# The state-space branch of a hybrid decoder block: two blocks of 128 steps scanned once, in place of sixteen blocks of 16 scanned twice

## The chip, the cores and the metric

The kernel runs on one core of a Trainium2 chip. The metric is the device time of one execution in microseconds (us). The core's engines are TensorE (PE in the rows, with its weight loads as PEld), VectorE (DVE), ScalarE (ACT), GpSimd (POOL) and SyncE (SP), which here issues the transfers. Each engine works through its own list of instructions in order and waits on semaphores for the others.

## The reference

For 256 tokens of width 2048 the block computes an RMS norm, one wide projection, two token mixers side by side, a gated merge, an output projection, and a mixture of experts with a final norm. The change touches one of the mixers, the state-space branch:

```
u = proj[:, :512]                       # 32 groups of 16 channels, 64 states each
lam_bar = exp(lam * step)               # complex, per state
bu = einsum(b_bar, u)                   # complex input of each state
s[t] = lam_bar * s[t-1] + bu[t]         # 256 steps
y = real(einsum(c, s)) + d * u
out = gelu(y) * sigmoid(gelu(y) @ w_glu + b_glu)
```

## The kernel before, in words

The 2048 states are 16 slices of 128 partitions, four slices to a chunk; `s5_chunk(c)` does one chunk. `lam_bar` is `rho` times a rotation. The kernel turns the input back by the rotation's angle, so that real and imaginary part become two real recurrences with factor `rho`, scans them on VectorE, and turns the result forward again. The tables of the angle reach 16 steps (`loc_c`, `loc_s`), and those of a block's angle 16 blocks (`blk_c`, `blk_s`); `powers` (L360) builds both by doubling.

A chunk works on two slices at a time (half a chunk). Per slice two small matmuls (L422) put the input into a `mid` bank of PSUM (two banks); six VectorE instructions of 256 elements (L430 to L435) turn it back into `bz`. A first scan (L444, real and imaginary, 512 elements each) runs inside each block of 16, with zeros in `d_loc` at each block's start. Eighteen instructions of 32 or 30 elements (L453 to L477) then work out what each block hands to the next, and add it to the blocks' first elements. The same scan runs a second time, six instructions of 512 elements turn the result forward (L483 to L488), and four matmuls (L493) take it to the outputs; each chunk ends with L495.

Around this stands the other mixer. In a loop of four batches of three heads, every projection unit is 1 MB of weights (`in_unit`, L398), of which ScalarE rounds each half (`whi`, L99) and VectorE takes the rest (`wlo`, L100); each half feeds 24 matmuls of 256 columns (L104 to L106), three for each block of weights. `lru_head` and `lru_tail` hold the second mixer's own VectorE, ScalarE and GpSimd work, `xl` (L536) among it, for which a matmul waits. After the loop come two more chunks, the projections by `w_plru` (L602, 36 matmuls a tile), by `w_in` (L613), `w_glu` and `w_ps5`, then `w_out` (L726) and the experts (L886 on), whose weights arrive by L704. Before the chunks, four pairs of transposes (L352) turn `bpad`, which VectorE builds (L341 to L345).

The order on every engine is fixed when the program is built: a scheduler with a clock of its own places the instructions, and the loads, roundings and differences of weights go ahead of all else (`high_priority`). The code's order decides only between the rest. A tile with one buffer makes its next user wait until the last reader is done.

Of the kernel before, what the change touches and what calls it, by code (L numbers as in the profile page):

```python
# [9 lines left out]
F32 = mybir.dt.float32  # L10
F32R = mybir.dt.float32r
# [24 lines left out]
def block_kernel(  # L36
# [268 lines left out]
    blk_c = tb_.tile([P, 16, LOC], F32, name="blk_c")  # L305
    blk_s = tb_.tile([P, 16, LOC], F32, name="blk_s")
# [53 lines left out]
    def powers(tc_, ts_):  # L360
        V.memset(tc_[:, :, 0], 1.0)
        V.memset(ts_[:, :, 0], 0.0)
        n = 1
        while n < 16:
# [12 lines left out]

    powers(loc_c, loc_s)
# [4 lines left out]
    V.tensor_tensor(rho16, rho, rho, op=ALU.mult)  # L383
    for _ in range(3):
        V.tensor_tensor(rho16, rho16, rho16, op=ALU.mult)
    d_loc = tb_.tile([P, 16, 16], F32, name="d_loc")
    d_blk = tb_.tile([P, 16, 16], F32, name="d_blk")
    V.tensor_copy(d_loc, rho[:, :, None].to_broadcast([P, 16, 16]))
    V.tensor_copy(d_blk, rho16[:, :, None].to_broadcast([P, 16, 16]))
    V.memset(d_loc[:, :, 0], 0.0)  # L390
    V.memset(d_blk[:, :, 0], 0.0)
# [16 lines left out]

    def s5_chunk(c):
        yps[c] = aux_bank()  # L410
        SB = 2
        for sb in range(4 // SB):
            bz = mp.tile([P, 2, SB, T], F32, tag="bz", bufs=2, name=nm("bz"))
            gz = mp.tile([P, 2, SB, T], F32, tag="gz", bufs=2, name=nm("gz"))
            s0 = 4 * c + sb * SB
            for i in range(SB):
                s = s0 + i
                q = s % 4
                rows = slice(32 * q, 32 * q + 32)
# [9 lines left out]
                bzv = bz[:, :, i, :].rearrange("p r (j t) -> p r j t", t=16)
                V.tensor_tensor(ttv[:, 0], p3[:, 1], ls, op=ALU.mult)  # L430
                V.tensor_tensor(ttv[:, 1], p3[:, 0], ls, op=ALU.mult)
                V.tensor_tensor(bzv[:, 0], p3[:, 0], lc, op=ALU.mult)
                V.tensor_tensor(bzv[:, 1], p3[:, 1], lc, op=ALU.mult)
                V.tensor_tensor(bz[:, 0, i, :], bz[:, 0, i, :], tt[:, 0], op=ALU.add)
                V.tensor_tensor(bz[:, 1, i, :], bz[:, 1, i, :], tt[:, 1], op=ALU.subtract)  # L435
            d3 = mp.tile([P, SB * T], F32, tag="d3", bufs=1, name=nm("d3"))
            A.activation(d3.rearrange("p (s j t) -> p s j t", s=SB, t=16),
                         d_loc[:, s0:s0 + SB, None, :].to_broadcast([P, SB, 16, 16]), AF.Copy)
            bz4 = bz.rearrange("p r s (j t) -> p r s j t", t=16)
            gz4 = gz.rearrange("p r s (j t) -> p r s j t", t=16)  # L440

            def scan():
                for ri in range(2):
                    V.tensor_tensor_scan(gz[:, ri].rearrange("p s t -> p (s t)"), d3,  # L444
                                         bz[:, ri].rearrange("p s t -> p (s t)"), 0.0, op0=ALU.mult, op1=ALU.add)

            scan()

            w = lambda: mp.tile([P, SB, 16], F32, tag="cw", bufs=8, name=nm("cw"))
            bc, bs = blk_c[:, s0:s0 + SB, 0:16], blk_s[:, s0:s0 + SB, 0:16]  # L450
            gr, gi = gz4[:, 0, :, :, 15], gz4[:, 1, :, :, 15]
            t1, t2, yr, yi, vr, vi = w(), w(), w(), w(), w(), w()
            V.tensor_tensor(yr, gr, bc, op=ALU.mult)  # L453
            V.tensor_tensor(t1, gi, bs, op=ALU.mult)
            V.tensor_tensor(yi, gi, bc, op=ALU.mult)
            V.tensor_tensor(t2, gr, bs, op=ALU.mult)
            V.tensor_tensor(yr, yr, t1, op=ALU.add)
            V.tensor_tensor(yi, yi, t2, op=ALU.subtract)
            fl = lambda t: t.rearrange("p s j -> p (s j)")
            db = fl(d_blk[:, s0:s0 + SB, :])  # L460
            V.tensor_tensor_scan(fl(vr), db, fl(yr), 0.0, op0=ALU.mult, op1=ALU.add)
            V.tensor_tensor_scan(fl(vi), db, fl(yi), 0.0, op0=ALU.mult, op1=ALU.add)
            bc, bs = blk_c[:, s0:s0 + SB, 1:16], blk_s[:, s0:s0 + SB, 1:16]
            v_r, v_i = vr[:, :, 0:15], vi[:, :, 0:15]
            t1, t2, yr, yi = w(), w(), w(), w()
            t1, t2, yr, yi = t1[:, :, 0:15], t2[:, :, 0:15], yr[:, :, 0:15], yi[:, :, 0:15]
            V.tensor_tensor(yr, v_r, bc, op=ALU.mult)
            V.tensor_tensor(t1, v_i, bs, op=ALU.mult)
            V.tensor_tensor(yi, v_i, bc, op=ALU.mult)
            V.tensor_tensor(t2, v_r, bs, op=ALU.mult)  # L470
            V.tensor_tensor(yr, yr, t1, op=ALU.subtract)
            V.tensor_tensor(yi, yi, t2, op=ALU.add)
            rb = rho[:, s0:s0 + SB, None].to_broadcast([P, SB, 15])
            V.tensor_tensor(yr, yr, rb, op=ALU.mult)
            V.tensor_tensor(yi, yi, rb, op=ALU.mult)
            V.tensor_tensor(bz4[:, 0, :, 1:16, 0], bz4[:, 0, :, 1:16, 0], yr, op=ALU.add)
            V.tensor_tensor(bz4[:, 1, :, 1:16, 0], bz4[:, 1, :, 1:16, 0], yi, op=ALU.add)  # L477
            scan()
            lc = loc_c[:, s0:s0 + SB, None, 0:16].to_broadcast([P, SB, 16, 16])
            ls = loc_s[:, s0:s0 + SB, None, 0:16].to_broadcast([P, SB, 16, 16])  # L480
            tr = mp.tile([P, SB, T], F32, tag="st", bufs=2, name=nm("so"))
            ti = mp.tile([P, SB, T], F32, tag="st", bufs=2, name=nm("so"))
            V.tensor_tensor(tr.rearrange("p s (j t) -> p s j t", t=16), gz4[:, 1], ls, op=ALU.mult)  # L483
            V.tensor_tensor(ti.rearrange("p s (j t) -> p s j t", t=16), gz4[:, 0], ls, op=ALU.mult)
            V.tensor_tensor(bz4[:, 0], gz4[:, 0], lc, op=ALU.mult)
            V.tensor_tensor(bz4[:, 1], gz4[:, 1], lc, op=ALU.mult)
            V.tensor_tensor(bz[:, 0], bz[:, 0], tr, op=ALU.subtract)
            V.tensor_tensor(bz[:, 1], bz[:, 1], ti, op=ALU.add)  # L488
            for i in range(SB):
                s = s0 + i  # L490
                q = s % 4
                for ri in range(2):
                    PE.matmul(yps[c][32 * q:32 * q + 32, :T], cp[:, s, ri, :], bz[:, ri, i, :],  # L493
                              start=(ri == 0), stop=(ri == 1), tile_position=(0, 32 * q))
        V.scalar_tensor_tensor(uT[:, c, :], uT[:, c, :], col(C_S5D, c), yps[c][:, :T], op0=ALU.mult, op1=ALU.add)  # L495
# [123 lines left out]
    y_hi = mp.tile([P, 4, T], F32R, tag="bz", bufs=2, name="y_hi")  # L619
    y_lo = mp.tile([P, 4, T], F32R, tag="gz", bufs=2, name="y_lo")  # L620
# [4 lines left out]
    for hf in range(2):  # L625
        hi, lo = split(raw[:, hf * 1024:(hf + 1) * 1024], 1024)
        for oo in range(2):
# [5 lines left out]
            tg = mp.tile([P, T], F32, tag="st", bufs=2, name=nm("tg"))  # L633
# [17 lines left out]
    for d4 in (3, 0, 1, 2):  # L651
        raw = load_unit(w_ps5[d4], 2048)
        for hf in range(2):
            hi, lo = split(raw[:, hf * 1024:(hf + 1) * 1024], 1024)
            for dd in range(2):
# [5 lines left out]
                tg = mp.tile([P, T], F32, tag="st", bufs=2, name=nm("tg"))  # L661
# [464 lines left out]
```

## Time and profile before

| what | value |
|---|---|
| median of three runs | 1090.77 us (1089.81 to 1092.85) |
| the profiled execution | 1093.92 us, span 1092.1 us |
| PE busy | 994.2 us (91%) |
| DVE busy | 645.6 us (59%) |
| ACT, POOL busy | 379.1 us, 75.6 us |
| transfers | 308.93 MB, mean 283 GB/s |

The profile cuts the span into 40 slices of 27.3 us. The mixers fill the first 19 or so, the experts the rest. Shares over the whole span mix the two, so each stage is read by itself. Matmuls are pipelined: a busy PE is one that always has a matmul under way, and its rate is read from the count of matmuls in a stretch.

### The profile page before, as it was taken

What the parts mean: (1) busy time and instruction counts of PE and PEld (TensorE: products, weight loads), DVE (VectorE), ACT (ScalarE), POOL (GpSimd) and SP (SyncE); (2) the same over time, 40 slices, a digit from 0 to 9 for tenths busy, and PEclk for the clock granted to TensorE, in tenths of its full rate; (3) what the DMA queues carried; (4) which work ended last, traced back from release to release, by engine and by line L of the source; (5) the groups of instructions that cost most, each with busy time, mean ns of one, the idle gap of its engine ahead of it and who ended that gap; (6) DMA issues with size and microseconds to landing.
All of it is one profiled execution on the core that took longest, in us unless ns stands there. A gap on an engine that the chain in (4) does not pass through costs nothing. (4 is left out here: it accounts for less than half of the span.)

```text
span 1092.1 us, 18171 instructions
## 1 busy us (share of the span) xinstructions
PE 994.2 (91%) x7435; PEld 749.4 (69%) x7435; DVE 645.6 (59%) x1356; ACT 379.1 (35%) x591; POOL 75.6 (7%) x76
## 2 busy tenths in 40 slices
PE   5999999999999999999999999999988979797872
PEld 5999899998989999998889945445443424343220
DVE  7899999999999964458544433333333312232225
ACT  5568547577633354445434110111110101011102
POOL 4001201223200000006000000000000000000000
PEclk9999999999999999999999999989998989999897
DMA  7655444454244555554979699999999999999991
GB/s 274 212 171 201 155 158 151 157 178 165 97 147 158 184 190 191 193 182 166 392 290 373 247 393 419 375 419 420 419 419 420 419 420 418 420 420 419 420 383 80
DMA packets 45164, 308.93 MB, mean 283 GB/s; under 512 B 5040, under 2 KB 6736, under 8 KB 9744
## 3 DMA queue, kind: packets, MB, share of 16 engines
q1 hardware_dynamic: 44784, 306.84, 72.5%
q8 instruction: 60, 0.98, 0.4%
q0 software_dynamic: 288, 0.85, 0.4%
q14 instruction: 32, 0.26, 0.1%
HBM read 305.57 MB, written 2.10 MB: 282 GB/s over the span
## 5 line engine op out<-in xcount | busy, mean ns | idle before, releaser
L100 DVE TENSOR_TENSOR wlo<-raw,whi 128x1024 fp32r<-128x1024 f32 (+1 forms) x194 | 230.2, 1189 | 98.0 <-ACT whi L99 97.6
L99 ACT ACTIVATE whi<-raw 128x1024 fp32r<-128x1024 f32 (+1 forms) x194 | 197.5, 1022 | 226.8 <-PE acc L105 163.5
L106 PE MATMUL acc<-hT_hi,wlo 128*128 128x256 f32 x848 | 238.8, 282 | 0.0
L105 PE MATMUL acc<-hT_lo,whi 128*128 128x256 f32 x848 | 238.8, 282 | 0.0
L104 PE MATMUL acc<-hT_hi,whi 128*128 128x256 f32 x848 | 238.2, 282 | 0.0
L990 DVE TENSOR_TENSOR once<-acc,once 128x512 f32<-128x512 f32 x128 | 79.8, 685 | 141.0 <-PE acc L986 141.0
L105 PEld LDWEIGHTS acc<-hT_lo,whi 128*128 128x128 f32 x848 | 159.6, 188 | 2.6 <-issue 2.6
L106 PEld LDWEIGHTS acc<-hT_hi,wlo 128*128 128x128 f32 x848 | 159.5, 188 | 2.1 <-issue 2.1
L104 PEld LDWEIGHTS acc<-hT_hi,whi 128*128 128x128 f32 x848 | 159.2, 188 | 2.4 <-issue 2.4
L104 PE MATMUL acc<-br,whi 128*128 128x256 f32 x336 | 95.9, 291 | 8.1 <-ACT br L177 7.7
L105 PE MATMUL acc<-br,whi 128*128 128x256 f32 x336 | 96.8, 290 | 2.4 <-DVE br L178 2.2
L106 PE MATMUL acc<-br,wlo 128*128 128x256 f32 x336 | 96.0, 290 | 2.2 <-DVE wlo L100 2.2
L986 PE MATMUL acc<-ysb,sct 32*128 32x512 f32 x512 | 95.9, 682 | 1.5 <-DVE once L990 0.8
L942 PE MATMUL mid<-eraw,once 128*32 128x512 f32 x512 | 66.0, 632 | 23.8 <-DMA eraw<-in_w_exp_dram 23.8
L918 PEld LDWEIGHTS aux<-sel,x 128*128 128x128 f32 x512 | 61.0, 195 | 31.0 <-issue 20.8
L974 PE MATMUL mid<-eraw,act 128*32 128x512 f32 x504 | 67.8, 658 | 10.2 <-DVE act L955 8.2
L942 PE MATMUL mid<-eraw,xTe 128*32 128x512 f32 x488 | 61.1, 616 | 16.5 <-DMA eraw<-in_w_exp_dram 16.5
L104 PEld LDWEIGHTS acc<-br,whi 128*128 128x128 f32 x336 | 65.7, 198 | 10.0 <-ACT br L177 7.7
L945 ACT ACTIVATE gus<-mid 128x512 f32<-128x512 f32 x32 | 19.1, 597 | 153.6 <-PE mid L942 153.6
L918 PE MATMUL aux<-sel,x 128*128 128x128 f32 x512 | 67.5, 285 | 5.3 <-DVE sct L967 5.3
L105 PEld LDWEIGHTS acc<-br,whi 128*128 128x128 f32 x336 | 66.1, 197 | 4.4 <-DVE br L178 2.7
L106 PEld LDWEIGHTS acc<-br,wlo 128*128 128x128 f32 x336 | 65.8, 197 | 4.0 <-DVE wlo L100 2.4
(352 smaller groups left out, 1307.0 us busy)
## 6 DMA issues: line engine op xcount, KB each, us to landing
eraw<-in_w_exp_dram SPq DMA_DIRECT2D x188, 1024.0 KB, 19.9
raw<-in_w_in_dram SPq DMA_DIRECT2D x59, 1024.0 KB, 4.9
raw<-in_w_out_dram SPq DMA_DIRECT2D x16, 1024.0 KB, 6.3
raw<-in_w_plru_dram SPq DMA_DIRECT2D x16, 768.0 KB, 4.2
raw<-in_w_ps_dram SPq DMA_DIRECT2D x4, 1024.0 KB, 5.0
once<-in_w_exp_dram SPq DMA_DIRECT2D x4, 1024.0 KB, 9.1
xt<-in_xT_dram SPq DMA_DIRECT2D x4, 512.0 KB, 8.7
x<-in_x_dram SPq DMA_DIRECT2D x2, 1024.0 KB, 7.5
```

Of the source, the lines that this page charges most:

```text
L99: A.activation(hi[:, :n], src, AF.Copy)
L100: V.tensor_tensor(lo[:, :n], src, hi[:, :n].bitcast(F32), op=ALU.subtract)
L104: PE.matmul(ps, whi, ahi, start=first, stop=False)
L105: PE.matmul(ps, whi, alo, start=False, stop=False)
L106: PE.matmul(ps, wlo, ahi, start=False, stop=last)
L918: PE.matmul(pt[:, kk * P:(kk + 1) * P], x1[h][:, k * P:(k + 1) * P], sel[b][:, h].rearrange("p e s -> p (e s)"), start=h == 0, stop=h == 1)
L942: mm = PE.matmul(ps[S * q:S * q + S, :], xT[e // B][:, 4 * j + q, es_], raw[:, q * 512:(q + 1) * 512], start=j == 0, stop=j == 3, tile_pos ...
L945: A.activation(gus[e], ps, AF.Copy)
L974: PE.matmul(ps[S * nb:S * nb + S, :], act[e][:, S * f:S * f + S], raw[:, bank(nb)], start=f == 0, stop=f == 1, tile_position=(0, S * nb))
L986: PE.matmul(sc[nb], sct[e][rows, h, :], ysb[e][rows, :], start=e == ex[0], stop=e == ex[-1], tile_position=(S * nb, 0))
L990: V.tensor_tensor(yacc[h][:, bank(nb)], sc[nb], old[:, bank(nb)], op=ALU.add)
```

## The change

The tables of the block's angle end at 8 blocks; `d_loc`, `d_blk` and the powers of `rho` go. A chunk takes its four slices together. It first builds the angle's cosine and sine for 128 steps (`fc`, `fs`: six VectorE instructions of 512 elements), and a tile of `rho` (`d3`, by ScalarE) whose first column GpSimd zeroes. The 256 steps are two blocks `j` of 128. Turning back takes two instructions of 512 elements per slice and two more for each pair of slices; each block is scanned once, real and imaginary; between the blocks five instructions of 4 or 8 elements add the first block's end, times `hop_c` and `hop_s`, to the second block's first element; turning forward takes, per block, two instructions of 1024 elements and two of 512. `bz` and `gz` hold a whole chunk and have one buffer each, where there were two of half the size. The temporaries of the later projections move from the tag `st` to `fc` and `fs`, `y_hi` and `y_lo` share one tile. The matmuls are as many as before.

```diff
-    powers(blk_c, blk_s)
-    rho16 = t16("rho16")
...
-    V.tensor_copy(d_loc, rho[:, :, None].to_broadcast([P, 16, 16]))
-    V.tensor_copy(d_blk, rho16[:, :, None].to_broadcast([P, 16, 16]))
...
+    powers(blk_c, blk_s, 8)
+    V.tensor_tensor(hop_c, rho, blk_c[:, :, 8], op=ALU.mult)
+    V.tensor_tensor(hop_s, rho, blk_s[:, :, 8], op=ALU.mult)
...
+    SB, HT = 4, T // 2
...
+        V.tensor_tensor(f4(fc), lc, bc, op=ALU.mult)
+        V.tensor_tensor(tt, ls, bs, op=ALU.mult)
+        V.tensor_tensor(f4(fc), f4(fc), tt, op=ALU.subtract)
+        V.tensor_tensor(f4(fs), ls, bc, op=ALU.mult)
+        V.tensor_tensor(tt, lc, bs, op=ALU.mult)
+        V.tensor_tensor(f4(fs), f4(fs), tt, op=ALU.add)
...
+        A.activation(d3, rho[:, gs_, None].to_broadcast([P, SB, HT]), AF.Copy)
+        G.memset(d3[:, :, 0], 0.0)
+        bz = mp.tile([P, 2, 2, SB, HT], F32, tag="bz", name=nm("bz"))
+        gz = mp.tile([P, 2, 2, SB, HT], F32, tag="gz", name=nm("gz"))
...
-            scan()
-            w = lambda: mp.tile([P, SB, 16], F32, tag="cw", bufs=8, name=nm("cw"))
...
-            scan()
...
+                V.tensor_tensor(tt[:, :, i - i0, :].rearrange("p r (j t) -> p r j t", t=HT), p3,
+                                fs[:, None, None, i, :].to_broadcast([P, 2, 2, HT]), op=ALU.mult)
+                V.tensor_tensor(bz[:, :, :, i, :].rearrange("p j r t -> p r j t"), p3,
+                                fc[:, None, None, i, :].to_broadcast([P, 2, 2, HT]), op=ALU.mult)
+            for ri in range(2):
+                o = bz[:, :, ri, i0:i0 + 2, :]
+                V.tensor_tensor(o, o, tt[:, 1 - ri].rearrange("p s (j t) -> p j s t", t=HT), op=ALU.subtract if ri else ALU.add)
+        for j in range(2):
+            for ri in range(2):
+                V.tensor_tensor_scan(f2(gz[:, j, ri]), f2(d3), f2(bz[:, j, ri]), 0.0, op0=ALU.mult, op1=ALU.add)
+            if j == 0:
...
+                V.tensor_tensor(m1, end, hop_c[:, None, gs_].to_broadcast([P, 2, SB]), op=ALU.mult)
+                V.tensor_tensor(m2, end, hop_s[:, None, gs_].to_broadcast([P, 2, SB]), op=ALU.mult)
+                o = bz[:, 1, :, :, 0]
+                V.tensor_tensor(o, o, m1, op=ALU.add)
...
+            V.tensor_tensor(tt, gz[:, j], fs[:, None].to_broadcast([P, 2, SB, HT]), op=ALU.mult)
+            V.tensor_tensor(bz[:, j], gz[:, j], fc[:, None].to_broadcast([P, 2, SB, HT]), op=ALU.mult)
+            for ri in range(2):
+                o = bz[:, j, ri]
+                V.tensor_tensor(o, o, tt[:, 1 - ri], op=ALU.add if ri else ALU.subtract)
```

The scheduler places everything anew. Two places on PE matter below. The first is where PE comes to the third chunk's output matmuls (L493 before, L470 now; `aux` is the bank of the outputs, `acc` that of a projection tile). In the kernel before, these are PE's rows there:

```order
L104 MATMUL acc_600_4171<-br3_87,whi_603_4194 128x256
L105 MATMUL acc_600_4171<-br3_87,whi_603_4194 128x256
L493 MATMUL aux_497_3653<-bz_498_3654,cp_611 32x256
L106 MATMUL acc_600_4171<-br3_87,wlo_604_4195 128x256
L104 MATMUL acc_600_4171<-br3_87,whi_603_4194 128x256
L105 MATMUL acc_600_4171<-br3_87,whi_603_4194 128x256
L106 MATMUL acc_600_4171<-br3_87,wlo_604_4195 128x256
L493 MATMUL aux_497_3653<-bz_498_3654,cp_611 32x256 x3
```

The bank `acc_600` is the first `w_plru` tile, and `bz_498` holds the first half of the chunk. In the changed kernel PE reads there:

```order
L104 MATMUL acc_523_3986<-br3_87,whi_526_4009 128x256
L470 MATMUL aux_452_3506<-bz_457_3519,cp_611 32x256
L105 MATMUL acc_523_3986<-br3_87,whi_526_4009 128x256
L106 MATMUL acc_523_3986<-br3_87,wlo_527_4010 128x256
L104 MATMUL acc_523_3986<-br3_87,whi_526_4009 128x256
L105 MATMUL acc_523_3986<-br3_87,whi_526_4009 128x256
L470 MATMUL aux_452_3506<-bz_457_3519,cp_611 32x256 x7
```

`acc_523` is the third `w_plru` tile and `bz_457` the whole chunk: the outputs of all four slices now come together, 97 matmuls behind the first `w_plru` matmul, where those of the first two slices came 32 behind it.

The second place is that of the first transposes (L352), in a unit of `w_in` for the fourth head. Before:

```order
L106 MATMUL acc_223_1716<-hT_hi_89,wlo_227_1746 128x256
L104 MATMUL acc_223_1716<-hT_hi_89,whi_226_1745 128x256
L105 MATMUL acc_223_1716<-hT_lo_90,whi_226_1745 128x256
L106 MATMUL acc_223_1716<-hT_hi_89,wlo_227_1746 128x256
L352 MATMUL aux_74_631<-ident_70,bpad_614 128x128
L352 MATMUL aux_75_635<-ident_70,bpad_614 128x128
```

And on PE in the changed kernel, where `acc_200` is the same unit's bank and `wlo_202` the first of its two halves:

```order
L106 MATMUL acc_200_1636<-hT_hi_89,wlo_202_1638 128x256
L104 MATMUL acc_200_1636<-hT_hi_89,whi_201_1637 128x256
L105 MATMUL acc_200_1636<-hT_lo_90,whi_201_1637 128x256
L106 MATMUL acc_200_1636<-hT_hi_89,wlo_202_1638 128x256
L352 MATMUL aux_74_631<-ident_70,bpad_614 128x128
L352 MATMUL aux_75_635<-ident_70,bpad_614 128x128
```

The transposes stand 18 matmuls earlier than they did.

## Rows read from the trace of the kernel before

**Rows 1.** The page's busy time, share of the span and instructions of each engine.

```profile
PE 994.2 (91%) x7435; PEld 749.4 (69%) x7435; DVE 645.6 (59%) x1356; ACT 379.1 (35%) x591; POOL 75.6 (7%) x76
```

**Rows 2.** By stretch: PE, PEld, DVE, ACT, POOL busy, clock, DMA share, GB/s.

```profile
100.00:400.00 300.00, 293.77 (x2303) 274.89 (x2303) 289.64 (x624) 168.86 (x244) 41.15 (x33) 0.99 0.47 160
400.00:480.00 80.00, 80.00 (x676) 80.00 (x676) 35.34 (x29) 34.78 (x42) 0.00 (x0) 1.00 0.55 187
310.00:316.00 6.00, 6.00 (x29) 4.41 (x28) 6.00 (x15) 0.84 (x1) 0.00 (x0) 0.72 0.39 131
700.00:1092.00 392.00, 319.88 (x2321) 144.07 (x2319) 125.41 (x281) 45.10 (x99) 1.09 (x2) 0.92 0.95 394
```

**Rows 3.** Waits of PE from 100 to 420 us: total us, times, longest.

```profile
PE aux L493 <- DVE bz L487: 2.6, 2, 2.2
PE aux L352 <- DVE bpad L345: 2.3, 1, 2.3
PE mid L105 <- DVE xl L536: 1.3, 1, 1.3
```

**Rows 4.** Groups of VectorE by form, 100 to 400 us: busy us, mean ns.

```profile
L444 DVE TENSOR_TENSOR_SCAN gz<-d,bz 128x512 f32<-128x512 f32 x32 | 39.2, 1261 | 0.0
L100 DVE TENSOR_TENSOR wlo<-raw,whi 128x1024 fp32r<-128x1024 f32 x65 | 79.9, 1232 | 0.4 <-ACT whi L99 0.2
L100 DVE TENSOR_TENSOR wlo<-raw,whi 128x768 fp32r<-128x768 f32 x32 | 30.6, 957 | 3.0 <-ACT whi L99 2.8
L434 DVE TENSOR_TENSOR bz<-bz,st 128x256 f32<-128x256 f32 x16 | 6.8, 425 | 0.0
L432 DVE TENSOR_TENSOR bz<-mid,loc_c 128x256 f32<-128x256 f32 x16 | 6.7, 419 | 0.0
L487 DVE TENSOR_TENSOR bz<-bz,so 128x512 f32<-128x512 f32 x8 | 5.5, 686 | 0.0
L453 DVE TENSOR_TENSOR cw<-gz,blk_c 128x32 f32<-128x32 f32 x8 | 2.6, 331 | 0.0
L467 DVE TENSOR_TENSOR cw<-cw,blk_c 128x30 f32<-128x30 f32 x8 | 1.5, 182 | 0.0
```

**Rows 5.** PE in order of time (start, us), from the last head to the third chunk.

```profile
279.30 0.81 PE L422 MATMUL mid<-uT,bt 32*128 32x256 f32 x3
280.04 0.38 PE L105 MATMUL mid<-xl,waxh 128*128 128x256 f32 x1
...
307.13 0.28 PE L105 MATMUL acc<-br,whi 128*128 128x256 f32 x1
309.59 0.62 PE L493 MATMUL aux<-bz,cp 128*32 128x256 f32 x2 [2.18 <-DVE bz L487]
```

**Rows 6.** VectorE in order of time over the same stretch.

```profile
278.28 0.41 DVE L536 TENSOR_TENSOR xl<-xc,xh 128x256 fp32r<-128x256 f32 x1
...
301.78 0.18 DVE L471 TENSOR_TENSOR cw<-cw,cw 128x30 f32<-128x30 f32 x1
...
302.47 2.34 DVE L444 TENSOR_TENSOR_SCAN gz<-d,bz 128x512 f32<-128x512 f32 x2
...
308.85 0.69 DVE L487 TENSOR_TENSOR bz<-bz,so 128x512 f32<-128x512 f32 x1
309.45 0.69 DVE L488 TENSOR_TENSOR bz<-bz,so 128x512 f32<-128x512 f32 x1
```

**Rows 7.** VectorE in order of time ahead of the transposes.

```profile
95.74 0.29 DVE L388 COPY d_loc<-rho 128x256 f32<-128x256 f32 x1
95.94 0.17 DVE L282 SCALAR_TENSOR_TENSOR rm<-e1eo,rm 128x16 f32<-128x16 f32 x1
...
114.82 1.21 DVE L100 TENSOR_TENSOR wlo<-raw,whi 128x1024 fp32r<-128x1024 f32 x1
115.95 0.21 DVE L371 TENSOR_TENSOR pt<-loc_s 128x64 f32<-128x64 f32 x1
```

**Rows 8.** SP in order of time: the first load of expert weights.

```profile
516.28 1.86 SPq L704 DMA_DIRECT2D eraw<-in_w_exp_dram  x2
```

More of the change, by code (lines that the diff above doesn't have):

```diff
@@ L304, in block_kernel @@
     loc_s = tb_.tile([P, 16, LOC], F32, name="loc_s")
-    blk_c = tb_.tile([P, 16, LOC], F32, name="blk_c")
-    blk_s = tb_.tile([P, 16, LOC], F32, name="blk_s")
+    blk_c = tb_.tile([P, 16, 9], F32, name="blk_c")
+    blk_s = tb_.tile([P, 16, 9], F32, name="blk_s")
     V.tensor_tensor(omc, sn, sn, op=ALU.mult)
@@ L358, in block_kernel, with powers @@
     pt2 = wk.tile([P, 16, 8], F32, name="pt2")
-    def powers(tc_, ts_):
+    def powers(tc_, ts_, top):
         V.memset(tc_[:, :, 0], 1.0)
@@ L363, in powers @@
         n = 1
-        while n < 16:
+        while n < top:
             bc = tc_[:, :, n:n + 1].to_broadcast([P, 16, n])
@@ L376, in powers @@
             n *= 2
-    powers(loc_c, loc_s)
+    powers(loc_c, loc_s, 16)
     V.tensor_copy(blk_c[:, :, 1], loc_c[:, :, 16])
     V.tensor_copy(blk_s[:, :, 1], loc_s[:, :, 16])
-    powers(blk_c, blk_s)
-    rho16 = t16("rho16")
[L383 to L387, printed above, removed]
-    V.tensor_copy(d_loc, rho[:, :, None].to_broadcast([P, 16, 16]))
-    V.tensor_copy(d_blk, rho16[:, :, None].to_broadcast([P, 16, 16]))
-    V.memset(d_loc[:, :, 0], 0.0)
-    V.memset(d_blk[:, :, 0], 0.0)
+    powers(blk_c, blk_s, 8)
+    hop_c = tb_.tile([P, 16], F32, name="hop_c")
+    hop_s = tb_.tile([P, 16], F32, name="hop_s")
+    V.tensor_tensor(hop_c, rho, blk_c[:, :, 8], op=ALU.mult)
+    V.tensor_tensor(hop_s, rho, blk_s[:, :, 8], op=ALU.mult)
     wks.close()
@@ L407, in in_unit @@
         return ps
+    SB, HT = 4, T // 2
     def s5_chunk(c):
         yps[c] = aux_bank()
[L411 to L419, printed above, removed]
+        gs_ = slice(SB * c, SB * c + SB)
+        fc = mp.tile([P, SB, HT], F32, tag="fc", name=nm("fc"))
+        fs = mp.tile([P, SB, HT], F32, tag="fs", name=nm("fs"))
+        t4 = lambda: mp.tile([P, 2, SB // 2, T], F32, tag="st", name=nm("st"))
+        tt = t4().rearrange("p r s t -> p (r s t)")[:, 0:SB * HT].rearrange("p (s j t) -> p s j t", s=SB, t=16)
+        f4 = lambda f: f.rearrange("p s (j t) -> p s j t", t=16)
+        sh = [P, SB, HT // 16, 16]
+        lc, ls = (l[:, gs_, None, 0:16].to_broadcast(sh) for l in (loc_c, loc_s))
+        bc, bs = (b[:, gs_, 0:HT // 16, None].to_broadcast(sh) for b in (blk_c, blk_s))
+        V.tensor_tensor(f4(fc), lc, bc, op=ALU.mult)
[4 more added lines that the diff above has]
+        V.tensor_tensor(f4(fs), f4(fs), tt, op=ALU.add)
+        d3 = mp.tile([P, SB, HT], F32, tag="d3", name=nm("d3"))
+        A.activation(d3, rho[:, gs_, None].to_broadcast([P, SB, HT]), AF.Copy)
+        G.memset(d3[:, :, 0], 0.0)
+        bz = mp.tile([P, 2, 2, SB, HT], F32, tag="bz", name=nm("bz"))
+        gz = mp.tile([P, 2, 2, SB, HT], F32, tag="gz", name=nm("gz"))
+        for i0 in range(0, SB, 2):
+            tt = t4()
+            for i in (i0, i0 + 1):
+                rows = slice(32 * i, 32 * i + 32)
                 ps = mid_bank()
@@ L429, in s5_chunk @@
[L429 to L445, printed above, removed]
@@ L457, in s5_chunk @@
[L457 to L473, printed above, removed]
@@ L482, in s5_chunk @@
[L482 to L494, printed above, removed]
+                              tile_position=(32 * i, 0))
+                p3 = ps.rearrange("p (r j t) -> p r j t", r=2, t=HT)
+                V.tensor_tensor(tt[:, :, i - i0, :].rearrange("p r (j t) -> p r j t", t=HT), p3,
+                                fs[:, None, None, i, :].to_broadcast([P, 2, 2, HT]), op=ALU.mult)
@@ new lines, in s5_chunk @@
+                V.tensor_tensor(bz[:, :, :, i, :].rearrange("p j r t -> p r j t"), p3,
[3 more added lines that the diff above has]
+                V.tensor_tensor(o, o, tt[:, 1 - ri].rearrange("p s (j t) -> p j s t", t=HT), op=ALU.subtract if ri else ALU.add)
+        f2 = lambda t: t.rearrange("p s t -> p (s t)")
+        for j in range(2):
+            for ri in range(2):
+                V.tensor_tensor_scan(f2(gz[:, j, ri]), f2(d3), f2(bz[:, j, ri]), 0.0, op0=ALU.mult, op1=ALU.add)
+            if j == 0:
+                w = lambda: mp.tile([P, 2, SB], F32, tag="cw", bufs=2, name=nm("cw"))
+                m1, m2 = w(), w()
+                end = gz[:, 0, :, :, HT - 1]
+                V.tensor_tensor(m1, end, hop_c[:, None, gs_].to_broadcast([P, 2, SB]), op=ALU.mult)
+                V.tensor_tensor(m2, end, hop_s[:, None, gs_].to_broadcast([P, 2, SB]), op=ALU.mult)
+                o = bz[:, 1, :, :, 0]
+                V.tensor_tensor(o, o, m1, op=ALU.add)
+                V.tensor_tensor(o[:, 0], o[:, 0], m2[:, 1], op=ALU.subtract)
+                V.tensor_tensor(o[:, 1], o[:, 1], m2[:, 0], op=ALU.add)
@@ new lines, in s5_chunk @@
+        for j in range(2):
+            tt = t4().rearrange("p r s t -> p (r s t)").rearrange("p (r s t) -> p r s t", r=2, s=SB)
+            V.tensor_tensor(tt, gz[:, j], fs[:, None].to_broadcast([P, 2, SB, HT]), op=ALU.mult)
[3 more added lines that the diff above has]
+                V.tensor_tensor(o, o, tt[:, 1 - ri], op=ALU.add if ri else ALU.subtract)
+        for i in range(SB):
+            for ri in range(2):
+                PE.matmul(yps[c][32 * i:32 * i + 32, :T], cp[:, SB * c + i, ri, :], bz[:, :, ri, i, :],
+                          start=(ri == 0), stop=(ri == 1), tile_position=(0, 32 * i))
@@ L616, in block_kernel @@
             A.activation(gs5[:, d, :], ps, AF.Tanh, bias=hcol(C_BGATE, d), scale=0.5)
-    y_hi = mp.tile([P, 4, T], F32R, tag="bz", bufs=2, name="y_hi")
-    y_lo = mp.tile([P, 4, T], F32R, tag="gz", bufs=2, name="y_lo")
+    y2 = mp.tile([P, 2, 4, T], F32R, tag="bz", name="y2")
+    y_hi, y_lo = y2[:, 0], y2[:, 1]
     A.activation(uT, uT, AF.Gelu_apprx_tanh)
```

24 lines of the change are left out of this document (2 added, 22 removed).

## The prediction

> **What bounds the kernel now.** I read the page's busy parts first, then busy time by stretch, then what PE waited for, and only then single instructions. The page gives PE 91% of the span and VectorE 59% [rows 1], which hides that the change lies in one stage. By stretch [rows 2], from 100 to 400 us both are nearly full: PE 293.8 of 300 us, VectorE 289.6. From 400 to 480 us, after the last chunk, PE is busy all the time and VectorE 35 of 80: there PE alone sets the pace, 676 matmuls in 80 us, 0.118 us each. From 700 us on the transfers run at 394 GB/s with a share of 0.95, and the end follows them. So the change can earn only what PE loses to VectorE between 100 and 400 us.
>
> PE's waits there [rows 3] are the whole list: 2.6 us for the turned output of a half chunk (L487, in two waits), 2.3 us for `bpad`, 1.3 us for `xl`; together 6.2 us, which agrees with the 6.2 us that PE is not busy in that stretch. After the longest wait, at 307 us, the granted clock was 0.72 on the mean from 310 to 316 us [rows 2]; at the two levels, 2.4 and 1.2 GHz, 6 us at 0.72 lose 1.7 us of work against full clock. All that can come back is 6.2 + 1.7 = 7.9 us.
>
> **The change part by part: VectorE's work.** Per chunk, before: 16 instructions of 256 elements out of PSUM at 0.419 and 8 in place at 0.425 make 10.1 us; 8 scans at 1.261 make 10.1; 12 instructions of 512 at 0.686 make 8.2; 36 small ones between 0.18 and 0.33 [rows 4], say 0.23, make 8.3. Sum 36.7 us. After: six of 512 for the angle, 4.1; eight of 512 out of PSUM and four in place, 8.2; four scans, 5.0; five tiny ones at 0.18, 0.9; four of 1024 at 1.232 (the row of `wlo`, the same size) and four of 512, 7.7. Sum 25.9. Over four chunks VectorE is relieved of some 43 us of its 645.6. The trace has no 512-element instruction that reads PSUM: one in place takes 0.686, and two of 256 out of PSUM 0.838; I take 0.686, since at 256 elements PSUM and SBUF differ by 0.006 us. The other end adds 0.15 x 32 = 4.9 us to VectorE and leaves 38.
>
> These 43 us are busy time, not gain. What PE gets is decided at the places where it waits, and there the order gives PE other work too.
>
> *The third chunk.* I count from the last head's `xl`, which stands before the chunk in both programs. Before, VectorE begins it at 278.28 and ends L487 at 309.54: 31.3 us [rows 6]. PE begins to use it at 280.04, 1.8 us later, and asks for the chunk at 307.25, after 27.2 us of work [rows 5]; 31.3 - 1.8 - 27.2 = 2.3, the wait that the row shows (2.18). Afterwards PE comes to the whole chunk, and the order has 72 more projection matmuls (8.5 us at 0.118) and four more input matmuls before it (each leaves two records; three records took 0.74 us from start to start [rows 5], so 2.0 us): 37.7 us. VectorE has to do more as well, because both halves are wanted at once. From start to start an instruction costs 0.09 less than its row says (L487 to L488: 0.60 apart, 0.69 long [rows 6]) and a small one 0.11 (six of them between 301.78 and 302.47). So the changed chunk up to the needed one costs 13 of 512 at 0.60, five at 0.1, and a tail of four of 1024 at 1.14 and three of 512 at 0.60, in all 14.7 us beside four scans. The half chunk before cost 12 x 0.33 + 18 x 0.11 + 5 x 0.60 = 9.0 us beside four scans. The difference is 5.7; three more splits of 768 columns lie between, 3 x 0.87 = 2.6. VectorE: 31.3 + 8.3 = 39.6; PE: 1.8 + 37.7 = 39.5. The wait falls from 2.2 to about 0.1, and the lowered clock behind it has no cause any more.
>
> *The second chunk.* Its wait of 0.4 us (2.6 less 2.2 [rows 3]) and the 1.3 us for `xl` shortly behind it belong to the time when VectorE finishes the second half of that chunk between the next heads' work. In the new order the chunk's output matmuls stand 121 projection matmuls earlier than its second half did, and nothing of the branch is left in front of that `xl`. I count both waits as gone. But VectorE still has 85% of its work in the stretch and the scheduler fits PE closely to it; for waits that come up at other places I set 0.6 us, between nothing and the 2.2 that one such place cost.
>
> *The transposes.* PE comes to them 18 matmuls earlier, 2.1 us. VectorE has nine instructions fewer in front of `bpad`: one split (1.13 us from start to start), two copies like L388 (0.20 each), four squarings (0.09 each), two memsets (0.03 each) [rows 7]: 1.9 us. The wait stays, 2.3 + 0.2.
>
> *The rest.* ScalarE makes `d3` four times instead of eight, and GpSimd sets its first column four times: both are ready long before a scan, since they need no input, and POOL is busy 41 of 300 us [rows 2]. The single `bz` makes a chunk's first product wait for the last matmul of the chunk in front; that is at the earliest a rival, below. The projections' temporaries keep two buffers in turn. On SP, the order of transfers from `w_plru` on is the same.
>
> **The sum.** Gone: 2.6 + 1.3 + 1.7 = 5.6 us. Come up: 0.2 + 0.6 = 0.8. The gain is 4.8 us at the end of the mixers. It reaches the end whole: the first load of expert weights goes out at 516.28, behind a load of `w_out` [rows 8], so what the transfers bound from then on starts earlier by as much. The profiled execution of 1093.92 us would become 1089.1; it stands 3.15 us above the median of the runs shown, so the median becomes 1090.77 - 4.8 = 1086.0.
>
> **The rivals.**
>
> *Nothing comes back, 1090.8.* PE is full at 98% between 100 and 400 us, and the scheduler may only trade one wait for another: it did place the matmuls later where VectorE got more to do at once. For it speaks that the third chunk's margin comes out at 0.1 us and not at 2; against it, that VectorE's load falls by a seventh in a stretch where all three waits were for VectorE. The Trainium skill says in "Perfetto Trace Analysis" (Identifying the Most-Contended Engine) that the engine with the highest occupancy is the one to work on first. By that rule, too, easing VectorE would return nothing, as PE is ahead on [rows 1]; but all of PE's list of waits names VectorE [rows 3], which speaks against it here.
>
> *Half comes back, 1088.2.* The wait for `bpad` grows to 3 us or more, since PE asks earlier, and the granted clock falls behind it as it fell behind the wait at 307 us: 5.6 - 1.7 - 0.7 - 0.6 = 2.6. Behind the 2.3 us wait for `bpad` before, the clock did not fall.
>
> *All comes back, 1082.9.* VectorE's 43 us make it run ahead everywhere, `bpad` included: 7.9 us.
>
> *Slower, 1097.1.* One buffer for `bz`: a chunk's first product (L441) stands in VectorE's queue until PE has done the output matmuls of the chunk in front. Behind it in that queue stand splits (`wlo`), which PE needs. At each of three handovers PE would then lose what it lost at 307 us, 2.2 and 1.7 us; 3 x 3.9 = 11.7, less the 5.6 gained, plus the 0.2 at `bpad`, is 6.3 us more. It decides where VectorE stands longer than PE has split weights in store: four halves of 24 matmuls, 11 us. No wait of that length is in sight, so it is unlikely.
>
> **How the numbers follow.** Forecast 0.50, everything back 0.12, half 0.14, nothing 0.15, slower 0.09. A change under 0.3%, 3.3 us, can't be told from none here; 1087.5 divides faster from the same. The forecast's own range is 1083.5 to 1088.3, most of it below that line: of its 0.50 I put 0.47 below the line, which with 0.12 for "everything" and 0.05 from "half" makes 0.64. The same takes "nothing" (0.15), the rest of "half" (0.09) and of the forecast (0.03), 0.27; slower 0.09. The range goes from below "everything" (1081.5, with the 1 us by which runs lie under the median) to just above "nothing" (1091.0).
>
> **What would show it.** In the changed profile: VectorE's busy time near 600 us; no wait over 0.5 us for the third chunk (L470) and no lowered clock behind it; a wait of 2 to 3 us at L352 still; the last output matmuls of the branch about 22 us earlier (191 projection matmuls fewer in front of them in the order, at 0.118); the first load of expert weights near 511.5 instead of 516.3. Wrong it would be if PE waits as long in sum as before, at new places, or if the mixers end earlier and the experts' stage gives it back.

## The result, and the profile after

The changed kernel takes 1083.38 us (median of six runs, 1080.64 to 1087.83) against 1091.78 for the kernel before beside it: 0.9925 of the time, 95% interval 0.9899 to 0.9951. In a second comparison it is 0.9918 (0.9898 to 0.9938). The forecast of 1086.0 lies 2.6 us above; the gain is 8.4 us and not 4.8. The profiled execution takes 1085.07 us, its span is 1083.3.

The page's busy parts, columns as in [rows 1]:

```profile
PE 983.0 (91%) x7435; PEld 748.5 (69%) x7435; DVE 620.7 (57%) x1164; ACT 377.6 (35%) x587; POOL 78.6 (7%) x80
```

VectorE is relieved of 24.9 us, not 43, and PE has as many matmuls as before but is busy 11 us less. The stretches that answer to [rows 2], and four short ones (columns: PE, PEld, DVE, ACT, POOL busy, clock, DMA share, GB/s):

```profile
100.00:400.00 300.00, 296.13 (x2367) 283.55 (x2366) 269.18 (x437) 170.93 (x244) 43.83 (x37) 0.98 0.49 166
700.00:1084.00 384.00, 305.40 (x2233) 137.28 (x2232) 121.05 (x275) 43.91 (x97) 1.10 (x2) 0.92 0.94 390
...
116.00:122.00 6.00, 4.90 (x30) 4.90 (x31) 5.94 (x14) 2.69 (x4) 0.33 (x1) 0.72 0.25 104
200.00:208.00 8.00, 8.00 (x50) 7.47 (x50) 8.00 (x13) 2.48 (x3) 0.00 (x0) 0.79 0.49 170
282.00:290.00 8.00, 8.00 (x43) 6.95 (x44) 7.74 (x16) 4.83 (x8) 3.62 (x4) 0.79 0.19 44
310.00:316.00 6.00, 6.00 (x52) 6.00 (x52) 6.00 (x9) 2.54 (x3) 0.10 (x1) 1.00 0.21 46
```

The lowered clock at 310 us is gone, as forecast. It comes up at three other places: behind the wait below, and at 202 and 284 us, where PE was busy all the time, shortly before with the small input matmuls (L436). PE's waits from 100 to 420 us, as [rows 3] (total us, times, longest):

```profile
PE aux L352 <- DVE bpad L345: 3.9, 1, 3.9
```

That is the whole list. Both waits for the turned output and the one for `xl` are gone (in the second profile, below, 0.5 us of it is left); the wait for `bpad` has grown from 2.3 to 3.9. SP's first load of expert weights, as [rows 8]:

```profile
508.69 1.86 SPq L681 DMA_DIRECT2D eraw<-in_w_exp_dram  x2
```

By this load, which I take as their end, the mixers end 7.6 us earlier (516.28 less 508.69), and the span is 8.8 us shorter: the experts' stage passed it all on. But the waits and the clock together can't make 7.6. The 100 to 400 us stretch gives 2.4 us of PE's idle time back and loses some 3.4 us to two more falls of the clock than before.

Most of the rest is in the output matmuls. PE in order of time round one half chunk of the kernel before (start, us; each matmul leaves two records):

```profile
162.53 0.28 PE L106 MATMUL acc<-hT_hi,wlo 128*128 128x256 f32 x1
162.74 0.62 PE L493 MATMUL aux<-bz,cp 128*32 128x256 f32 x2
163.29 0.39 PE L104 MATMUL acc<-hT_hi,whi 128*128 128x256 f32 x1
163.51 0.28 PE L105 MATMUL acc<-hT_lo,whi 128*128 128x256 f32 x1
...
163.84 1.06 PE L493 MATMUL aux<-bz,cp 128*32 128x256 f32 x6
164.83 0.38 PE L104 MATMUL acc<-hT_hi,whi 128*128 128x256 f32 x1
```

and round the whole first chunk of the changed kernel:

```profile
180.63 0.62 PE L470 MATMUL aux<-bz,cp 128*32 128x256 f32 x2
181.18 0.39 PE L104 MATMUL acc<-hT_hi,whi 128*128 128x256 f32 x1
...
181.85 1.08 PE L470 MATMUL aux<-bz,cp 128*32 128x256 f32 x14
182.86 0.38 PE L105 MATMUL acc<-hT_lo,whi 128*128 128x256 f32 x1
```

One matmul holds PE for 0.55 us from start to the next start, three in a row for 0.99, and seven in a row for 1.01. Before, a chunk is twice 1 + 3 matmuls, 3.08 us; now it is 1 + 7, 1.56. Four chunks: 12.3 against 6.2 us (the trace of before has 12.7, as one group fell into the lowered clock). The neighbours pay too: the projection matmul in front of a group and the one behind it take 0.21 and 0.22 us to the next start, in place of the usual 0.12. With 16 groups that is some 3.2 us, with 8 half of it. In sum some 8 us of PE's time went away that no wait showed. With 2.4 us of waits gained and 3.4 lost to the clock, about 1 us of the 7.6 stays without an owner.

### The profile page after: what moved, and what is told of

The parts are those of the page before. It is cut to its first block, busy times and chain, and to the rows that moved or that the text cites. A ratio compares the mean times of both kernels' runs of the same rounds, so it can differ in the third digit from the quotient of the medians.

```text
span 1083.3 us, 17997 instructions
## 1 busy us (share of the span) xinstructions
PE 983.0 (91%) x7435; PEld 748.5 (69%) x7435; DVE 620.7 (57%) x1164; ACT 377.6 (35%) x587; POOL 78.6 (7%) x80
## 5 line engine op out<-in xcount | busy, mean ns | idle before, releaser
L100 DVE TENSOR_TENSOR wlo<-raw,whi 128x1024 fp32r<-128x1024 f32 (+1 forms) x194 | 232.6, 1202 | 113.8 <-ACT whi L99 113.6
L105 PEld LDWEIGHTS acc<-hT_lo,whi 128*128 128x128 f32 x848 | 161.8, 191 | 2.1 <-issue 2.1
L106 PEld LDWEIGHTS acc<-hT_hi,wlo 128*128 128x128 f32 x848 | 161.7, 191 | 1.7 <-issue 1.7
L963 PE MATMUL acc<-ysb,sct 32*128 32x512 f32 x512 | 93.2, 671 | 1.5 <-DVE once L967 0.8
L951 PE MATMUL mid<-eraw,act 128*32 128x512 f32 x504 | 63.1, 618 | 12.7 <-DVE act L932 11.6
L895 PE MATMUL aux<-sel,x 128*128 128x128 f32 x512 | 69.7, 290 | 3.3 <-DVE sct L944 3.3
```

The lines of the kernel that those rows point to most:

```text
L100: V.tensor_tensor(lo[:, :n], src, hi[:, :n].bitcast(F32), op=ALU.subtract)
L105: PE.matmul(ps, whi, alo, start=False, stop=False)
L106: PE.matmul(ps, wlo, ahi, start=False, stop=last)
L895: PE.matmul(pt[:, kk * P:(kk + 1) * P], x1[h][:, k * P:(k + 1) * P], sel[b][:, h].rearrange("p e s -> p (e s)"), start=h == 0, stop=h == 1)
L951: PE.matmul(ps[S * nb:S * nb + S, :], act[e][:, S * f:S * f + S], raw[:, bank(nb)], start=f == 0, stop=f == 1, tile_position=(0, S * nb))
L963: PE.matmul(sc[nb], sct[e][rows, h, :], ysb[e][rows, :], start=e == ex[0], stop=e == ex[-1], tile_position=(S * nb, 0))
```

## The experiments

*Theory (grouping)*: most of the gain is that the output matmuls of a chunk, which go to four column tiles of 32, now stand in one group. *Rival (relief)*: the gain is VectorE's 25 us, as the prediction has it. The scheduler made a third thing matter: a small edit in the mixers can let it order the experts' stage anew. I compared that order on PE and VectorE kernel by kernel; letters in this table mark equal orders. The loads are SP's first and its 99th of the 188 loads of expert weights in the profile (us); the last column is the time between them. Where an expectation speaks of the last load, it is this 99th.

| kernel | ratio to before (95%) | order | first load | 99th load | between |
|---|---|---|---|---|---|
| before | 1 | A | 516.28 | 820.88 | 304.6 |
| changed | 0.9925 (0.9899 to 0.9951) | B | 508.69 | 811.66 | 303.0 |
| changed, again | 0.9918 (0.9898 to 0.9938) | B | 506.74 | 811.94 | 305.2 |
| b_group | 0.9978 (0.9953 to 1.0004) | C | 509.02 | 816.37 | 307.4 |
| b_group, again | 1.0021 (0.9998 to 1.0043) | C | 509.08 | 815.89 | 306.8 |
| b_riout | 0.9976 (0.9955 to 0.9997) | D | 510.62 | 817.70 | 307.1 |
| b_group_o | 0.9926 (0.9904 to 0.9948) | A | 505.81 | 810.46 | 304.7 |
| a_pairs | 0.9972 (0.9949 to 0.9996) | A | 512.73 | 815.65 | 302.9 |
| a_scan2 | 0.9953 (0.9930 to 0.9976) | B | 512.40 | 816.45 | 304.1 |
| a_riout | 0.9874 (0.9842 to 0.9905) | E | 504.58 | 807.59 | 303.0 |
| a_riout, again | 0.9900 (0.9870 to 0.9930) | E | 503.58 | 808.78 | 305.2 |
| a_ri_late | 0.9907 (0.9878 to 0.9935) | E | 501.64 | 804.22 | 302.6 |
| a_ri_late, again | 0.9870 (0.9839 to 0.9901) | E | 501.35 | 806.99 | 305.6 |

From the first load to the 188th it is 526.4 to 529.3 us in the orders A, B and E, 530.4 and 532.3 in C, and 530.7 in D.

**Grouping without relief (b_group).** The kernel before, the matmuls of both halves issued when the second is ready:

```diff
+            halves.append((s0, bz))
+        first = None
+        for s0, bz in reversed(halves):
+            with tc.issue_after(first) if first is not None else ExitStack():
-            for i in range(SB):
+                for i in range(SB):
...
+                        first = first or mm
```

> The kernel before with one edit: the output matmuls of a chunk's two halves are issued together, once the second half is ready (one matmul, then seven in a row, as in the changed kernel). VectorE's work is that of before. Grouping theory (the changed kernel gains mostly because output matmuls to four column tiles in a row cost PE half of what two groups of four cost): the 64 records take PE 6 to 7 us from start to start in place of 12.7, and the kernel is 4 to 7 us faster than before (ratio 0.9935 to 0.9965) although VectorE stays at 645 us. Relief theory (the gain comes from VectorE's 25 us): no gain, ratio 0.999 or more, and waits for the outputs as long as before or longer, since PE wants both halves at once.

The output matmuls took 6.25 us from start to start, as the theory has it, and the mixers ended 7.3 us earlier. The time did not follow: 0.9978 does not show a gain. The profile loses it behind the mixers. Stretch 670 to 690 us of this kernel:

```profile
670.00:690.00 20.00, 19.60 (x98) 7.69 (x100) 6.31 (x12) 1.42 (x3) 0.00 (x0) 0.83 0.80 316
```

The loads run at 316 GB/s there. Is that chance?

> The kernel before with the output matmuls of a chunk grouped (1 + 7), once more, unedited. Its first profile left the mixers 7.3 us earlier than before but ended only 2.9 us earlier: at 681 us the granted clock was down for 6.8 us and the loads of experts' weights fell 6 us behind. If that fall belongs to the program, it stands there again and the ratio stays near 0.998. If it is chance of one execution, it is gone, the span ends 6 to 8 us before that of the kernel before, and the ratio of many runs, in which such chances even out, should be nearer to 0.995 than to 0.998. The mixers' part is to repeat: output matmuls 6.25 us, first load of experts' weights near 509 us.

The mixers repeated (509.08) and the fall of the clock at 681 us was gone, yet the 99 loads took 306.8 us and the ratio was 1.0021. So an experts' stage that is 2 to 3 us longer belongs to this program, and b_riout, whose order there differs from before's too, shows it as well. What makes this order slower I did not follow further.

> The kernel before with the output matmuls of a chunk's two halves issued together and, in each half, the real parts of both slices before the imaginary parts, so that two column tiles take turns. VectorE's work is that of before. If matmuls to different column tiles run beside each other, the 64 records take 4 to 6 us from start to start in place of 12.7 (6.25 with the grouping alone), the mixers end 7 to 9 us earlier than before and the kernel is 4 to 9 us faster (ratio 0.992 to 0.9965), without any relief of VectorE. If grouping is worth nothing in the time, the ratio is 0.998 or more.

The ratio of 0.9976 misses the expected range, and the mixers ended 5.7 us earlier, not 7 to 9. Its output matmuls took 6.2 us, not less than with the grouping alone: the scheduler cut the eight into 2 + 6, and in the six, two column tiles still get two matmuls each. The six on PE:

```profile
194.36 1.07 PE L498 MATMUL aux<-bz,cp 128*32 128x256 f32 x12
195.36 0.39 PE L104 MATMUL acc<-hT_hi,whi 128*128 128x256 f32 x1
```

**The same grouping with the old order of the experts (b_group_o).** Against b_group, the slices go in reverse within each half; that alone keeps the order of the experts' stage as it was:

```diff
-                for i in range(SB):
+                for i in reversed(range(SB)):
```

> The kernel before with the output matmuls of a chunk grouped (1 + 7) as in the earlier run, but within each half the slices in reverse order. That detail leaves the order of the experts' stage on PE and VectorE as it is in the kernel before; in the earlier grouped kernel the scheduler had placed that stage anew, and its loads of experts' weights took 307 us from first to last (two profiles) in place of 304.6. If the grouping is worth its 6.5 us and the new order of the experts took 3 us back, the first load goes out near 509 us, the last one near 812 to 814 us (303 to 305 us later), and the ratio is 0.993 to 0.9965. If the grouping's gain is lost in the experts' stage whatever the order there, the stage takes 307 us again and the ratio is 0.998 or more.

Its row for the same stretch:

```profile
670.00:690.00 20.00, 18.98 (x119) 9.08 (x114) 5.99 (x14) 1.64 (x4) 0.00 (x0) 0.83 0.97 378
```

At the same granted clock the loads run at 378 GB/s, the 99 loads take 304.7 us, and the ratio is 0.9926: as much as the whole change gives. Yet VectorE does the work of before, and PE still waits 4.5 us for it, against 6.2 before. Stretch 100 to 400 us and waits from 100 to 420 us of this kernel:

```profile
100.00:400.00 300.00, 295.48 (x2380) 281.51 (x2379) 292.01 (x624) 172.05 (x247) 50.47 (x33) 1.00 0.48 166
```

```profile
PE aux L352 <- DVE bpad L345: 2.4, 1, 2.4
PE mid L105 <- DVE xl L542: 1.7, 3, 0.7
PE mid L423 <- DVE bz L434: 0.4, 1, 0.4
```

VectorE is busy 292.0 of 300 us, no less than the 289.6 before [rows 2]. The mixers end 10.5 us earlier: some 6.5 by the matmuls, 1.6 by their neighbours, 1.7 by waits, and up to 1.7 by the clock, which is full here throughout; these parts make 1 us more than the whole. With this order of the experts, the grouping is shown to be worth the gain by itself; with b_group's it gained nothing that the times show. A part of that is waiting: the wait for the turned output, 2.6 us before, is gone though VectorE is no faster, since PE asks for a chunk's outputs only once. How much of the way from b_group to here the order of the experts made isn't shown: b_group's mixers also end 3.2 us later, and in both its profiles the clock falls at 343 us.

**Relief without grouping (a_pairs).** The changed kernel, turned forward and taken to the outputs two slices at a time:

```diff
+        for i0 in range(0, SB, 2):
...
-        for i in range(SB):
+            for i in (i0, i0 + 1):
```

> The changed kernel with one edit: turning forward and the output matmuls are done for two slices, then for the other two (1 + 3 matmuls twice per chunk, as in the kernel before); VectorE does eight instructions more per chunk of half the size each, some 1 to 2 us a chunk. Grouping theory: the output matmuls take PE 12 to 13 us again in place of 6.25, and the kernel gives back 5 to 7 us against the changed one (ratio to before 0.997 to 0.999). Relief theory: within 1 us of the changed kernel (ratio 0.992 to 0.9935), as VectorE is still 20 us below before.

VectorE's busy time is 621.6 us, the output matmuls take 12.3 us again, and the order of the experts is that of before. PE's waits from 100 to 420 us:

```profile
PE aux L352 <- DVE bpad L345: 3.8, 1, 3.8
```

The mixers end 3.6 us earlier than before, and the ratio of 0.9972 is 3.1 us: this is the relief alone. Against the changed kernel (0.9922, the mean of its two comparisons) it gives back 0.0050, 5.5 us, as the grouping theory expected.

**Relief taken back (a_scan2).**

```diff
-                V.tensor_tensor_scan(f2(gz[:, j, ri]), f2(d3), f2(bz[:, j, ri]), 0.0, op0=ALU.mult, op1=ALU.add)
+                for _ in range(2):
+                    V.tensor_tensor_scan(f2(gz[:, j, ri]), f2(d3), f2(bz[:, j, ri]), 0.0, op0=ALU.mult, op1=ALU.add)
```

> The changed kernel with each of its 16 scans done twice into the same tile: 16 x 1.3 = 21 us more on VectorE, which takes back most of the 25 us by which it was relieved; the matmuls and their grouping stay. Grouping theory with little worth to the relief: 0 to 2 us slower than the changed kernel (ratio to before 0.9925 to 0.9945), output matmuls still 6 to 7 us. Relief theory: waits of PE for VectorE of 3 to 6 us come up between 100 and 400 us, and the kernel is 4 to 8 us slower than the changed one (ratio 0.996 to 1.000).

Between the two theories' ranges, in neither: 0.9953 is 0.0031 or 3.4 us slower than the changed kernel, with the same order of the experts. PE's waits from 100 to 420 us now have four lines more:

```profile
PE acc L106 <- DVE wlo L100: 2.7, 4, 1.0
PE acc L105 <- DVE br L541: 0.6, 1, 0.6
PE mid L105 <- DVE xl L514: 0.4, 1, 0.4
PE mid L104 <- ACT xh L513: 0.4, 1, 0.4
```

So 17 us of VectorE's work (637.6 against 620.7 busy) bring 4.1 us of waits. Both experiments put the relief at some 3 us.

**Four column tiles in turn (a_riout).**

```diff
-        for i in range(SB):
-            for ri in range(2):
+        for ri in range(2):
+            for i in range(SB):
```

> The changed kernel with the two loops round the output matmuls exchanged: the four column tiles take turns (real part of all four slices, then imaginary part), where two matmuls in a row went to the same tile. If matmuls to different column tiles run beside each other, as the grouping theory has it, the 64 records take 4 to 6 us from start to start in place of 6.25 and the kernel is 0 to 2 us faster than the changed one. If the gain of the grouping comes only from fewer changes between kinds of matmul, nothing changes: within 1 us of the changed kernel.

The output matmuls take 4.4 us in all, 1.8 less. The ratios of 0.9874 and, later, 0.9900 are 5.2 and 2.4 us under the changed kernel, more than that, though the intervals overlap; the mixers end 3 to 4 us earlier than in the changed one's two profiles on the mean. The experts' order is another one here (E, not B), so not all of it need come from the matmuls. PE round the first chunk, and at the second, whose eight were not cut:

```profile
180.17 0.64 PE L470 MATMUL aux<-bz,cp 128*32 128x256 f32 x8
180.74 0.39 PE L104 MATMUL acc<-hT_hi,whi 128*128 128x256 f32 x1
181.05 0.64 PE L470 MATMUL aux<-bz,cp 128*32 128x256 f32 x8
181.62 0.39 PE L105 MATMUL acc<-hT_lo,whi 128*128 128x256 f32 x1
...
237.07 1.07 PE L470 MATMUL aux<-bz,cp 128*32 128x256 f32 x16
238.07 0.39 PE L105 MATMUL acc<-hT_lo,whi 128*128 128x256 f32 x1
```

Four matmuls to four tiles hold PE for 0.57 us, one held it for 0.55: they run beside each other. The Trainium skill says in "TensorE: Matmul & The Clock Gate" (Why this matters for your kernels) that small outputs placed in distinct column groups run concurrently, 2.38 times as fast for three tiles at 512 columns; these rows agree. In all the runs the time of a group goes by the most matmuls that one tile gets in it: 0.54 to 0.57 us for one, 0.98 to 1.02 for two at full clock, whether the group has three, six, seven or eight. The order inside a group makes no difference (seven in pairs 1.01, eight in turn 1.00). It matters where the scheduler cuts: 1 + 7 in pairs leaves two matmuls to a tile in the seven, 0.55 + 1.01 us; 4 + 4 in turn leaves one to a tile in each part, 2 x 0.57.

**The second profile of the changed kernel.**

> The changed kernel once more, unedited, for a second profile. In its first profile the granted clock fell at 202 and 284 us with no wait ahead, which cost the mixers 3 us. If these falls belong to the program, they stand at the same places again and the first load of experts' weights goes out near 508.7 us. If they are chance of one execution, they are gone or elsewhere, and that load goes out 2 to 4 us earlier, near 505 to 507 us. The fall behind the wait for bpad (at 116.7 us) should be there in both cases. The ratio to before should come out at 0.990 to 0.995 again.

Two of the three falls were chance. The same stretches as above:

```profile
200.00:208.00 8.00, 8.00 (x61) 7.30 (x60) 8.00 (x13) 2.53 (x4) 0.00 (x0) 1.00 0.53 185
282.00:290.00 8.00, 8.00 (x57) 7.08 (x58) 8.00 (x17) 6.04 (x9) 4.08 (x4) 1.00 0.29 97
```

Without them the mixers end at 506.74, 9.5 us before those of the kernel before. PE's waits are 3.8 us for `bpad` and 0.5 for `xl`. The fall behind the wait for `bpad` is there again, at 117.5 us.

**The wait for bpad (a_ri_late).** On a_riout, the transposes wait for a later unit's first half, and the pool of `bpad` is closed later:

```diff
+            if b == 1 and i == 0:
+                with tc.issue_after(half_mm[0]):
+                    turn_b()
+                wks.close()
+                mp = mps.enter_context(tc.tile_pool(name="mp", bufs=1, side="right", reuse_waits="tile"))
+                s5_chunk(0)
```

> The changed kernel with the four column tiles in turn (0.9874 of before in its own run) and one more edit: the transposes of bpad, and the first chunk with them, are held back on PE until half of a later unit is through, 81 projection matmuls (9.6 us) later, so that VectorE has bpad ready. If the 4.0 us wait and the lowered clock behind it (3.4 us at half speed, 1.7 us of work) are what they cost, this gives 4 to 6 us more: ratio 0.982 to 0.984, no wait for bpad, no lowered clock near 117 us. If PE only meets VectorE later at another place (the first chunk's work starts 9.6 us later, with less margin up to its outputs), waits of 2 to 4 us come up between 150 and 200 us and the ratio stays at 0.986 to 0.988.

The wait and the fall behind it are gone, and only two short waits come up. Its waits from 100 to 420 us, and two stretches:

```profile
PE acc L106 <- DVE wlo L100: 0.9, 1, 0.9
PE mid L104 <- ACT xh L517: 0.4, 1, 0.4
```

```profile
100.00:400.00 300.00, 298.55 (x2423) 285.61 (x2422) 269.17 (x439) 173.14 (x247) 48.78 (x37) 1.00 0.49 169
...
116.00:122.00 6.00, 5.05 (x42) 4.81 (x41) 5.91 (x15) 5.00 (x7) 0.00 (x0) 1.00 0.28 91
```

The mixers end 2.9 us earlier than in a_riout, less than the 4 to 6 expected. The ratio of 0.9907 is outside both expected ranges and could not tell the two kernels apart, so both ran once more on one chip:

> The changed kernel with the column tiles in turn, once more, unedited, on the same chip as the kernel with the late transposes. Its ratio to before should be 0.985 to 0.991 again, and the fall of the clock behind the wait for bpad should stand near 116 us.

> The changed kernel with the column tiles in turn and the transposes 81 projection matmuls later, once more, unedited. The order of the experts' stage is that of the kernel it is compared with, so only the mixers differ. If the wait for bpad and the clock behind it are worth what the first profile showed (mixers' end 2.9 us earlier), its median lies 2 to 4 us below the other's in this call. If the experts' stage takes that back, the two agree within 1 us.

Medians 1082.75 and 1079.27 us: 3.5 us less, as expected, though the two intervals overlap (0.9870 to 0.9930, 0.9839 to 0.9901); the mixers end 2.2 us earlier. By the medians, a_ri_late is the fastest kernel here and beats both given ones. By the ratios of two comparisons each, 0.9889 and 0.9887 on the mean, it and a_riout are level.

## Why the prediction was right in its sign and short in its size

- *VectorE's 43 us* were 25. The step that failed is the sum by durations. VectorE's instructions overlap: six small ones of 0.18 to 0.21 us stand 0.11 apart [rows 6], and I counted 0.23 each. By starts, with 0.33, 1.14, 0.60 and 0.11 for the kinds before (28.2 us a chunk) and 0.60, 1.14, 1.13 and 0.1 for those after (22.8), four chunks give 21.6. I had used these distances for the third chunk and not for the sum. The 43 us set the price of the rival "all comes back" and are no term of the 4.8.
- *The third and the second chunk, and `xl`*: right. All three waits, 3.9 us, are gone, with and without the grouping (a_pairs), and the clock no longer falls at 311 us. But the relief is not the only cause that does it: with the grouping alone (b_group_o) the wait for the turned output and that fall are gone too.
- *The transposes*: +0.2 was +1.6. PE asks 2.4 us earlier (forecast 2.1), but VectorE has `bpad` ready only 0.9 earlier and not 1.9. It stood idle for ScalarE in front of it:

```profile
106.05 0.42 DVE L533 SCALAR_TENSOR_TENSOR pb<-a,pb 128x256 f32<-128x256 f32 x1 [1.48 <-ACT pb L563]
```

  And the clock falls behind the longer wait. This is the rival "half comes back", down to its condition; it did happen. The relief alone ended the mixers 3.6 us earlier in a_pairs, nearer to that rival's 2.6 than to the 4.8 forecast.
- *"The matmuls are as many as before"*, and so at no cost: this is the term that was missing. They cost 6.25 us in place of 12.7, since the order writes them in one group of seven, and their neighbours some 1.6 less. With it the bound failed, that all that can come back is 7.9 us: it took PE's own work as fixed. The trace of before had the warning (0.55 for one, 0.99 for three, not three times as much), and the regrouping stood in the order that I showed; the price of seven in a row stood in no row of before.
- *Passed on whole*: right for the change, by 303.0 and 305.2 us for the 99 loads against 304.6. It is not a rule: with b_group's new order of the experts they took 2.5 us more.
- *VectorE is the limit, by PE's waits*: only half true. VectorE decides the waits, but the larger gain was fewer microseconds of PE's own work. The Trainium skill's rule in "Perfetto Trace Analysis" (Identifying the Most-Contended Engine), to work on the busiest engine first, was weighed against the waits and set aside; for the larger part of the gain it named the right engine, by these runs. The Trainium skill has TensorE judged there by its FLOPs and weight loads and not by its matmuls' busy share; by the weight loads, 69% against VectorE's 59% [rows 1], PE is ahead as well.
- *The signs named*: VectorE at 600 us was 620.7, the first load at 511.5 was 508.69, the wait of 2 to 3 us at L352 was 3.9, the last output matmuls came 31 us earlier and not 22; no wait at L470 and no lowered clock behind it was right.

That the time fell into the range is in part luck. Waits and clock, the only terms of the forecast, gave 2.4 and lost 3.4 us in the first profile and gave some 2 in the second, where 4.8 was forecast; the output matmuls, which were no term, made up for it.

The two gains do not add up: 0.9926 (grouping) and 0.9972 (relief) would make 0.990, the change has 0.992. They share the wait for the turned output and the fall behind it, which either takes away alone; the intervals allow both values. Open also is the time of b_group: its 188th load of expert weights stood 4.3 and 6.1 us before that of the kernel before, its time not at all. Its two profiled executions, 1090.87 and 1087.63 us, lie below its medians of 1092.16 and 1094.75, so the profiles don't show what the others lost. One clue is on record: its 24 executions had a granted clock of 0.957 on the mean, 52 of the kernel before beside them 0.961, b_group_o's ten 0.961, and its two profiled ones 0.963 and 0.969. Whether the lower clock is the cause isn't shown.

## What to carry to other kernels

Count what a regrouping does to matmuls that use part of the array: in these runs their cost went by groups, and in a group by the most matmuls that one column tile got, not by number; where a group may be cut, tiles should take turns. Price overlapping instructions by the distance of their starts. Where a scheduler places all work, look at whether an edit also moved a stage that it did not mean to touch before reading its ratio as the edit's worth.

## What the runs showed of the hardware

Column-tiled matmuls: one in 0.55 us, four to four tiles in 0.57, seven of which pairs share a tile in 1.01, eight to four tiles in 1.00. The full-array matmuls next to such a group took 0.21 and 0.22 us to the next start in place of 0.12. The granted clock was 0.79 on the mean from 200 to 208 and from 282 to 290 us in one execution, with PE busy throughout, and 1.00 in the next one of the same program. Behind the wait for `bpad` it fell to 1.2 GHz in all six profiles where that wait was 3.8 to 4.0 us, and in two (b_group, b_riout) of the five where it was 2.3 or 2.4. A VectorE instruction of 512 elements takes as long from PSUM as from SBUF: L439 reads PSUM, L467 SBUF (100 to 400 us; busy us, mean ns).

```profile
L439 DVE TENSOR_TENSOR st<-mid,fs 128x512 f32<-128x512 f32 x16 | 10.9, 680 | 0.5 <-PE mid L436 0.3
L467 DVE TENSOR_TENSOR bz<-bz,st 128x512 f32<-128x512 f32 x16 | 10.3, 679 | 0.0
```
